# The head of one diffusion layer written out by hand, with tokens 0-767 ahead of the others

## The chip, the cores and the metric

The kernel runs on one core of a Trainium2 chip. A core has five engines with an instruction queue each: TensorE (PE, matmuls and transposes; its weight loads are listed as PEld), VectorE (DVE), ScalarE (ACT), GpSimd (POOL) and SyncE (SP), which here issues most of the DMA transfers. SBUF is the memory on the chip, 128 partitions wide; PSUM holds what TensorE writes. The metric is the device time of one execution in microseconds, lower is better.

## The reference

One inference step of a layer, on 1024 latent tokens and 128 context tokens with 1024 channels, all in fp32:

```python
mod = silu(c) @ w_ada + b_ada          # one row for latent, one for context tokens: sh1, sc1, ga1, sh2, sc2, ga2
h = rmsnorm(x, g1) * (1 + sc1) + sh1
u, q, k, v, g = split(h @ w_in)        # 512, 1024, 256, 256, 2048 columns
m = sigmoid(g_f) * (fourier_mix(u) @ w_fo) + sigmoid(g_a) * (attention(q, k, v, cache, sink) @ w_ao)
x = x + ga1 * (m @ w_out)
h = rmsnorm(x, g2) * (1 + sc2) + sh2
x = x + ga2 * (square(relu(h @ w_ff1)) @ w_ff2)     # 4096 hidden channels
y = rmsnorm(x, final_g)
```

Attention reads a window of 128 tokens to either side and the cached context keys; context tokens read only each other. The outputs are y for both kinds of tokens and the new keys and values.

## The kernel before

The tokens are nine tiles of 128: tiles 0 to 7 are latent, tile 8 is context. The 1024 channels are eight chunks of 128. A product in fp32 is made of three matmuls on operands that are split into a high and a low part (high by high, high by low, low by high); a split is an ACT cast (L147 and others) and a DVE subtraction (L142).

**The head.** The nine x tiles are loaded by SP (L408, 512 KB each), squared and summed on ACT (L410) and normalised in groups of three (the small steps L177 to L183, then the multiplications L417 on DVE and L415 on POOL). TensorE transposes each tile in eight pieces of 128 x 128 (L422), which ACT and DVE copy out of PSUM (L423). Then, chunk by chunk (`make_h`): the chunk's columns of `w_ada` are loaded in two halves (L401), multiplied by silu(c) on TensorE (L436 for chunk 0 in one fp32 piece, L449 for the others, split), the result row is copied (L458), turned into columns by four small matmuls (L462, "fold"), the bias is added on DVE (L464, L467), and the chunk of all 1152 tokens is modulated on ACT (L471), cast (L472) and its low part subtracted (L142). Projection round 1 multiplies tiles 0 to 5 by the first 512 columns of `w_in` chunk by chunk (L233 to L235, 144 matmuls of 512 columns); round 2 does tiles 6 to 8, after the results of round 1 have been copied out (L365). Here a scheduler sets the order of each engine's queue, by data dependences and estimated costs.

**The middle.** Projections, the Fourier mixer and attention follow, in an order written out by hand (`tc.manual_schedule`). Meanwhile the other modulation chunks are made a piece at a time and added up on DVE (L282) into `mods`, which holds them with the channel on the partition.

**The modulation rows.** The gate vectors ga1 and ga2 are wanted as rows along the free axis on all partitions. `ga_rows` (L1238) writes them from `mods` to a DRAM buffer `ga_d`, two channel chunks at a time, eight transfers on POOL's queue for each gate; each transfer writes single fp32 elements. It is called for ga1 ahead of the seam, and for ga2 at unit 12 of the first MLP matmul (FF1); the scheduler lets each transfer go when its part of `mods` is ready. `ga_put` (L1359) loads a row spread over 128 partitions.

**The seam.** Between w_out and the MLP each tile is finished in steps: `fin_a` multiplies the output by ga1, adds it to the residual row in one of three buffers `XS[t % 3]`, stores that row to DRAM and sums its squares (L1427 to L1434); `fin_b1`, `fin_b2` make the reciprocal root; `fin_b3` scales the row on ACT (L1461); `fin_c` transposes it (L1473) and modulates it (L1478 on ACT, L1480 on DVE). Tile 5 is scaled in place in `XS[2]`. Pieces of other work (`part`, `ev_part`, `t_hi`, `t_lo`) are dealt between these steps in a written order.

**FF1.** Units of weights of 2 x 512 KB are loaded through SP (L1379) into two rotating buffers, split on ACT and DVE, and multiplied (L1684 to L1686); the results go to DRAM through SP as well (L1356), so loads and stores stand in one queue.

## Time and profile before

| what | value |
|---|---|
| median of 3 runs (lowest to highest) | 1657.26 us (1656.18 to 1659.58) |
| profiled execution | 1654.63 us, span 1652.9 us |
| mean granted TensorE clock | 0.995 |
| busy PE / DVE / ACT / POOL | 1610.2 / 1127.1 / 884.8 / 273.1 us |
| DMA | 290.19 MB, mean 176 GB/s |
| first transpose of the head | at 11.51 us |
| first matmul of projection round 2 | at 86.86 us |

The profiled execution is one run under the hardware profiler; the span goes from its first to its last instruction. A row of the timeline gives start, duration, engine, line, operation, operands, and in brackets the engine's idle time before it with what released it. A matmul's duration overlaps the next one's, so the distance between starts is its price in a sequence. The granted clock is the share of full speed at which TensorE was allowed to run in a stretch.

### The profile page before, as it was taken

Reading aid. Unit: us, or ns where it says so; the run is one execution under the profiler, and the core shown is the slowest. Engines: PE = TensorE matmul, PEld = TensorE weight load, DVE = VectorE, ACT = ScalarE, POOL = GpSimd, SP = SyncE. Lnnn points to the kernel's source line nnn. Section 1 sums busy time; section 2 is a strip of 40 time slices with the busy share of each in tenths; the row PEclk is TensorE's granted clock in tenths of the full one; section 3 lists DMA queues with packets and bytes.
Section 4 is the critical chain, followed back from the end, with each engine's and each line's share of the span. In section 5 each row is a group of like instructions: output and inputs, shape, how many; then the busy total and the mean of one; then the engine's idle time right before and its main releaser. Section 6 shows DMA issues by size and latency. Waiting matters only on the chain.

```text
span 1652.9 us, 24756 instructions
## 1 busy us (share of the span) xinstructions
PE 1610.2 (97%) x8357; PEld 1412.5 (85%) x8357; DVE 1127.1 (68%) x2215; ACT 884.8 (54%) x1722; POOL 273.1 (17%) x399
## 2 busy tenths in 40 slices
PE   6999999999999999999999999999999999999998
PEld 5789889899889999889988888887888888888887
DVE  7644266867767865678658877766776588785764
ACT  7743455777677665564346564444445354444542
POOL 1020252555445332310000000000000200000000
PEclk9999999999999999999999999999999999999999
DMA  8342578556444333587575335445555995666841
GB/s 322 129 121 87 182 215 216 132 119 162 121 125 114 106 106 112 160 285 237 161 288 178 117 138 183 163 146 143 166 146 180 348 375 176 197 202 188 257 155 64
DMA packets 217351, 290.19 MB, mean 176 GB/s; under 512 B 27540, under 2 KB 142164, under 8 KB 217096
## 3 DMA queue, kind: packets, MB, share of 16 engines
q1 hardware_dynamic: 205768, 269.72, 52.6%
q0 software_dynamic: 11456, 18.90, 4.0%
q8 instruction: 66, 1.08, 0.3%
q14 instruction: 61, 0.50, 0.1%
HBM read 205.10 MB, written 83.44 MB: 175 GB/s over the span
## 4 chain that ended last, share of the span: by engine, by line
PE 74%; DVE 5%; DMA 3%; ACT 2%; issue 1%; SPq 0%; DVEq 0%; ACTq 0%
PE x L2083 6%; PE x L2085 6%; PE x L2084 6%; PE x L1684 5%; PE x L1686 5%; PE x L1685 5%; PE mm L195 4%; PE mm L197 4%; PE mm L196 4%; PE ptp L859 3%; PE x L197 2%; PE x L195 2%; PE x L196 2%; PE s L819 2%; PE s L820 2%; PE o L874 2%
## 5 line engine op out<-in xcount | busy, mean ns | idle before, releaser
L142 DVE TENSOR_TENSOR wlo<-wraw,whi 128x1024 fp32r<-128x1024 f32 x96 | 121.4, 1266 | 97.8 <-ACT whi L147 75.2
L833 ACT ACTIVATE pt<-pt,mx 128x513 f32<-128x513 f32 (+2 forms) x144 | 95.8, 666 | 82.9 <-DVE mx L821 64.5
L196 PE MATMUL mm<-BR,whi 128*128 128x384 f32 x408 | 137.1, 336 | 0.0
L2084 PE MATMUL x<-BR 128*128 128x512 f32 (+1 forms) x348 | 132.9, 382 | 0.0
L2085 PE MATMUL x<-BR 128*128 128x512 f32 (+1 forms) x348 | 132.5, 382 | 0.0
L2083 PE MATMUL x<-BR 128*128 128x512 f32 (+1 forms) x348 | 131.4, 382 | 0.0
L195 PE MATMUL mm<-BR,whi 128*128 128x384 f32 x360 | 128.1, 356 | 2.9 <-ACT z L717 1.6
L821 DVE CUSTOM_DVE_ANT_0 pt<-s,mask,nsink 128x512 f32<-128x512 f32 (+2 forms) x144 | 96.7, 673 | 40.4 <-PE s L820 38.2
L845 POOL TENSOR_SCALAR pt<-pt,mx 128x512 f32<-128x512 f32 (+2 forms) x144 | 94.8, 670 | 177.5 <-DVE mx L843 175.7
L197 PE MATMUL mm<-BR,wlo 128*128 128x384 f32 x360 | 121.6, 338 | 0.0
L147 ACT CAST whi<-wraw 128x1024 fp32r<-128x1024 f32 x62 | 64.9, 1049 | 100.1 <-DMA wraw<-in_w_ff_dram 53.7
L2056 ACT CAST BR<-aa 128x512 fp32r<-128x512 f32 x80 | 49.7, 621 | 105.5 <-PE x L2084 51.4
L142 DVE TENSOR_TENSOR pl<-ptp,ph 128x512 fp32r<-128x512 f32 x124 | 83.8, 687 | 23.1 <-ACT ph L862 21.7
L326 POOL TENSOR_TENSOR macc<-macc,mprod 128x512 f32<-128x512 f32 x70 | 93.7, 1338 | 7.7 <-ACT macc L324 2.5
L196 PEld LDWEIGHTS mm<-BR,whi 128*128 128x128 f32 x408 | 77.1, 189 | 6.0
L859 PE MATMUL ptp<-ident,pt 128*128 128x128 f32 x496 | 74.4, 274 | 4.0 <-DVE pl L142 3.9
L142 DVE TENSOR_TENSOR BR<-aa,BR 128x512 fp32r<-128x512 f32 x80 | 55.2, 690 | 33.2 <-ACT BR L2056 32.7
L862 ACT CAST ph<-ptp 128x512 fp32r<-128x512 f32 x124 | 70.5, 585 | 12.5 <-PE ptp L859 11.2
L195 PE MATMUL mm<-BT,whi 128*128 128x384 f32 x216 | 76.8, 356 | 0.0
L2084 PEld LDWEIGHTS x<-BR 128*128 128x128 f32 x348 | 65.4, 188 | 12.9
L2083 PEld LDWEIGHTS x<-BR 128*128 128x128 f32 x348 | 65.4, 188 | 12.9
L2085 PEld LDWEIGHTS x<-BR 128*128 128x128 f32 x348 | 65.4, 188 | 12.6
(470 smaller groups left out, 4792.8 us busy)
## 6 DMA issues: line engine op xcount, KB each, us to landing
aa<-hr_d SPq DMA_DIRECT2D x108, 256.0 KB
ab<-in_w_ff_dram SPq DMA_DIRECT2D x108, 256.0 KB
hr_d<-ZR SPq DMA_DIRECT2D x104, 256.0 KB
wraw<-in_w_in_dram SPq DMA_DIRECT2D x41, 512.0 KB
wraw<-in_w_ff_dram SPq DMA_DIRECT2D x34, 512.0 KB
mraw<-in_w_ada_dram SPq DMA_DIRECT2D x96, 128.0 KB
z_d<-z SPq DMA_DIRECT2D x48, 192.0 KB
q_d<-qt SPq DMA_DIRECT2D x48, 192.0 KB
```

The costliest lines, as they stand in the source:

```text
L142: return eng.tensor_tensor(dst, raw, hi.bitcast(F32), ALU.subtract)
L195: nc.tensor.matmul(out, ah, bh, start=start, stop=False)
L196: nc.tensor.matmul(out, ah, bl, start=False, stop=False)
L197: return nc.tensor.matmul(out, al, bh, start=False, stop=stop).ins
L326: nc.gpsimd.tensor_tensor(acc, acc, pr_, ALU.add)
L821: nc.vector.tensor_tensor_reduce(out=pt[:, e, :n], in0=sp[:, :n], in1=mask[:, m0 : m0 + n], scale=-0.125, scalar=nsink[:, h0 + e : h0 + e ...
L833: nc.scalar.activation(pt[:, e, : n + 1], pt[:, e, : n + 1], AF.Exp, bias=mx[:, e : e + 1], scale=-1.0, accum_out=mx[:, 2 + e : 3 + e],)
L845: ins = nc.gpsimd.tensor_scalar(pt[:, e, :n], pt[:, e, :n], mx[:, 4 + e : 5 + e], 1.0, ALU.mult, ALU.mult)
L859: nc.tensor.transpose(pst[:, h * P : (h + 1) * P], u["pts"][h // 2][:, h % 2, b * P : (b + 1) * P], ident)
L2083: nc.tensor.matmul(ps, xh, bh, start=start, stop=False, skip_group_check=cont)
L2084: nc.tensor.matmul(ps, xh, bl, start=False, stop=False, skip_group_check=cont)
L2085: nc.tensor.matmul(ps, xl, bh, start=False, stop=stop, skip_group_check=cont)
```

## The change

1. **Head.** The loops are replaced by a list of steps in a written order for PE, ACT, DVE and SP. Tiles 0 to 5 go first: their six x tiles and the weights for chunks 0 to 2 are loaded ahead of tiles 6 to 8, the x buffers go from nine to six, and silu's copies (`put_c`) stand behind the first loads. The modulation of chunk 0 starts ahead of the first transpose. Tokens 0-767 are modulated, split and multiplied chunk by chunk; for chunk 0 in two pieces of 384. Tiles 6 to 8 are transposed within chunks 3 to 5, and tokens 768-1151 are modulated on POOL (`h3`), split and left for round 2 at the end of chunks 5 and 6. Tiles 4 and 5 are normalised on POOL, and so are 6 to 8.
2. **Modulation rows.** `ga_rows` turns eight chunks by two transposes on TensorE, copies the 8 x 256 result on ACT and writes it with one transfer on SP.
3. **Seam.** Tile 5's scaled row goes to `XS[1]` instead of in place; row 8 is loaded before row 7; tile 7's `fin_b3` moves up ahead of `ev_part` and `fin_c(6)`; `fin_c(7, 0)` takes its PSUM bank from another pool; some `part`, `t_hi` and `t_lo` pieces change places.
4. **Context step.** In `step_ctx` the eight matmuls with the low part of the tokens follow the sixteen others instead of standing between them.

The number of projection, modulation and transposing matmuls is the same, but for the four new transposes of part 2. Lines below are those of the kernel before (L3xx to L19xx) or of the changed one, as marked.

TensorE at the start of the head, before (`x` is a PSUM bank, `xt` an x tile, `wada` modulation weights, `mr` the modulation row; x2 or x4 counts equal rows):

```order
L422 MATMUL x_152<-ident,xt_130 128x128 x4
L422 MATMUL x_158<-ident,xt_130 128x128 x4
...
L422 MATMUL x_244<-ident,xt_198 128x128 x4
L436 MATMUL mm_310<-wada_311,siluc 2x256 x4
L436 MATMUL mm_310<-wada_313,siluc 2x256 x4
L422 MATMUL x_272<-ident,xt_250 128x128 x4
...
L422 MATMUL x_304<-ident,xt_258 128x128 x4
L462 MATMUL mm_325<-ident,mr_323 128x2 x2
L449 MATMUL mm_335<-whi_340,crep 128x256
```

The same in the changed kernel:

```order
L478 MATMUL mm_176<-wada_128,siluc 2x256 x4
L427 MATMUL x_182<-ident,xt_122 128x128 x4
...
L427 MATMUL x_200<-ident,xt_124 128x128 x4
L478 MATMUL mm_176<-wada_130,siluc 2x256 x4
L427 MATMUL x_210<-ident,xt_126 128x128 x4
L427 MATMUL x_215<-ident,xt_126 128x128 x4
L496 MATMUL mm_233<-ident,mr_231 128x2 x2
L427 MATMUL x_248<-ident,xt_132 128x128 x4
...
L427 MATMUL x_281<-ident,xt_134 128x128 x4
L525 MATMUL x_288<-whi_265,BR 128x512
```

The modulation of chunk 0 now brackets the first two tiles, its fold stands behind three tiles instead of nine, and the first projection matmul behind five.

DVE in the changed head, from the multiplication of tile 2 to the low part of the first tokens (`rs_` are the small steps of the reciprocal root):

```order
L457 TENSOR_SCALAR xt_126<-xt_126,rs_r_168 128x1024
...
L488 COPY mr_231<-mm_176 2x256
L500 TENSOR_SCALAR mods<-mm_233,cols 128x2 x2
L501 TENSOR_SCALAR s_94<-mods,cols 128x2
L448 RECIPROCAL rs_a_226<-rs_a_226 128x2
...
L457 TENSOR_SCALAR xt_132<-xt_132,rs_r_227 128x1024
L443 TENSOR_SCALAR rs_v_258<-ssq 128x1
L431 COPY xnT<-x_210 128x4x128
L508 TENSOR_SCALAR xnT<-xnT,s_94,mods 128x384
...
L142 TENSOR_TENSOR wlo_266<-wraw_138,whi_265 128x1024
L142 TENSOR_TENSOR BR<-xnT,BR 128x384
```

In this order tile 3's multiplication stands behind the modulation of chunk 0, and the first projection's low parts behind both.

ACT in the seam around tile 7, before (L1461 scales tile 7, L1478 modulates, L1363 casts, L1714 copies a result):

```order
L1446 ACTIVATE rsw_10107<-rsw_10107 128x1
L1714 COPY ZR<-x_10121 128x384
L1478 ACTIVATE ZR<-mm_10140,mods,s_95 128x128 x4
L1363 CAST BR<-ZR 128x512
L1461 ACTIVATE ZR<-ZR,rsw_10107 128x1024
L1363 CAST BR<-ZR 128x512
```

The changed kernel (L1668 scales):

```order
L1653 ACTIVATE rsw_10146<-rsw_10146 128x1
L1668 ACTIVATE ZR<-ZR,rsw_10146 128x1024
L1921 COPY ZR<-x_10160 128x384
L1685 ACTIVATE ZR<-mm_10180,mods,s_95 128x128 x4
L1570 CAST BR<-ZR 128x512 x2
```

The scaling has moved ahead of a copy, four modulations and a cast.

SP in FF1 of the changed kernel, around the second row store (L1563 stores results, L1586 loads weights):

```order
L1586 DMA wraw_12693<-in_w_ff_dram 128x4x256
L1965 DMA hc_d<-ZR 128x512
L1563 DMA hr_d<-ZR 128x512 x2
L1446 DMA ga_d<-ZR 8x2x128
L1586 DMA wraw_12695<-in_w_ff_dram 128x4x256
L1563 DMA hr_d<-ZR 128x512 x7
L1965 DMA hc_d<-ZR 128x512
L1586 DMA wraw_12862<-in_w_ff_dram 128x4x256
L1586 DMA wraw_12864<-in_w_ff_dram 128x4x256
```

The row store, which was on POOL's queue, stands between two stores and a weight load.

The diff, cut to its core:

```diff
@@ -401,79 +399,286 @@
...
+            def h_id(m, r, vec=None):
+                for a, b, tok in ((r.start, min(r.stop, 1024), 0), (max(r.start, 1024), r.stop, 1)):
+                    if a < b:
+                        x, sc, sh = xnT[:, m, a:b], s1[:, m, tok : tok + 1], mod(0, m, tok)
+                        if vec:
+                            vec.tensor_scalar(x, x, sc, sh, ALU.mult, ALU.add)
+                        else:
+                            nc.scalar.activation(x, x, AF.Identity, bias=sh, scale=sc)
+
+            def h_hi_(m, r):
+                nc.scalar.copy(h_hi[m][:, r], xnT[:, m, r])
+
+            def h_lo_(m, r):
+                sub(nc.vector, h_lo[m][:, r], xnT[:, m, r], h_hi[m][:, r])
+
...
+            R0, R1, R6, R3 = slice(0, 384), slice(384, 768), slice(0, 768), slice(768, NT)
+            ET = mybir.EngineType
+            mh = ExitStack()
+            mh.enter_context(tc.manual_schedule(engines={ET.PE, ET.Activation, ET.DVE, ET.SP}))
+            px = {}
+
+            def xTs(t):
+                for hh in range(2):
+                    px[t, hh] = xT(t, hh, bank6)
+
+            def xevs(t, engs):
+                for hh in range(2):
+                    if engs[hh] != "-":
+                        xev(t, hh, px[t, hh], engs[hh])
+
+            for t in range(3):
+                x_load(t)
+            wada_load(0)
+            for t in range(3, 6):
+                x_load(t)
+            win_load(0)
+            wada_load(1)
+            wada_load(2)
+            win_load(2)
+            put_c()
+            for t in range(3):
+                square(t)
+            rs_a(0, 3)
+            rs_b(0, 3)
+            ada_mv(0, (0,))
+            xmul(0)
+            xTs(0)
+            square(3)
+            xmul(1)
+            xTs(1)
+            ada_mv(0, (1,))
+            xmul(2)
+            xTs(2)
+            xevs(0, "va")
+            square(4)
+            xev(1, 0, px[1, 0], "v")
+            rs_a(3, 2)
+            xev(1, 1, px[1, 1], "a")
+            mod_row(0, True)
+            mod_col(0)
+            square(5)
+            rs_b(3, 2)
+            xmul(4, nc.gpsimd)
+            xmul(3)
+            xTs(3)
+            rs_a(5, 1)
+            xevs(2, "va")
+            win_hi(0)
+            h_id(0, R0, nc.vector)
+            h_hi_(0, R0)
+            rs_b(5, 1)
+            xmul(5, nc.gpsimd)
+            xTs(4)
+            win_lo(0)
+            h_lo_(0, R0)
+            u_mm(0, (0,))
+            ada_hi(1, 0)
+            xevs(3, "aa")
+            ada_lo(1, 0)
+            xTs(5)
+            u_mm(0, (1, 2))
+            ada_hi(1, 1)
+            ada_lo(1, 1)
+            xevs(4, "aa")
+            xevs(5, "va")
+            ada_hi(2, 0)
+            h_id(0, R1, nc.vector)
+            h_hi_(0, R1)
+            h_lo_(0, R1)
+            ada_lo(2, 0)
+            ada_mv(1)
+            mod_row(1)
+            ada_hi(2, 1)
+            for t in range(6, NTT):
+                x_load(t)
+            u_mm(0, (3,))
+            mod_col(1)
+            u_mm(0, (4, 5))
+            h_id(1, R6)
+            h_hi_(1, R6)
+            ada_lo(2, 1)
+            h_lo_(1, R6)
+            ada_mv(2)
+            win_hi(2)
+            win_lo(2)
+            wada_load(3)
+            win_load(4)
+
+            def h3(m):
+                h_id(m, R3, nc.gpsimd)
+                h_hi_(m, R3)
+                h_lo_(m, R3)
+
+            for k in range(1, KC):
+                n = k + 1
+                more = n + 1 < KC
+                tl = k + 3 if k in (3, 4, 5) else None
+                if n < KC:
+                    mod_row(n)
+                u_mm(k, (0,))
+                if n < KC:
+                    mod_col(n)
+                if more:
+                    ada_hi(n + 1, 0)
+                    ada_lo(n + 1, 0)
+                u_mm(k, (1, 2))
+                if tl:
+                    ta = xT(tl, 0, mmt)
+                u_mm(k, (3,))
+                if tl:
+                    tb = xT(tl, 1, mmt)
+                u_mm(k, (4, 5))
+                if n < KC:
+                    h_id(n, R6)
+                    h_hi_(n, R6)
+                if tl:
+                    xev(tl, 0, ta, "a")
+                if more:
+                    ada_hi(n + 1, 1)
+                if n < KC:
+                    h_lo_(n, R6)
+                if tl:
+                    xev(tl, 1, tb, "v")
+                if more:
+                    ada_lo(n + 1, 1)
+                    ada_mv(n + 1)
+                if k in (2, 4):
+                    win_hi(k + 2)
+                    win_lo(k + 2)
+                if k == 2:
+                    win_load(6)
+                if k + 3 < KC:
+                    wada_load(k + 3)
+                if k == 1:
+                    square(6)
+                    square(7)
+                if k == 2:
+                    square(8)
+                    rs_a(6, 3)
+                    rs_b(6, 3)
+                    for t in range(6, NTT):
+                        xmul(t, nc.gpsimd)
+                if k == 5:
+                    h3(0)
+                if k == 6:
+                    for m in range(1, KC):
+                        h3(m)
+            mh.close()
@@ -1233,12 +1438,14 @@
     fbank[0] = gt
 
     def ga_rows(k, row):
+        pr = fold_bank[0]()
         for tok in range(2):
-            for m in range(0, 8, 2):
-                nc.gpsimd.dma_start(
-                    ga_d[row + tok, m * P : (m + 2) * P].rearrange("(m p) -> p m", p=P),
-                    mods[:, k * 8 + m : k * 8 + m + 2, tok],
-                )
+            nc.tensor.transpose(pr[:8, tok * P : (tok + 1) * P], mods[:, k * 8 : k * 8 + 8, tok], ident)
+        rows = zh(3)[:8, : 2 * P]
+        nc.scalar.copy(rows, pr[:8, : 2 * P])
+        nc.sync.dma_start(
+            ga_d[row : row + 2].rearrange("t (m p) -> m t p", p=P), rows.rearrange("m (t p) -> m t p", t=2)
+        )
 
     def ga_load(pool, row, tag):
         out = []
@@ -1457,7 +1664,7 @@
     def fin_b3(t, n=1):
         rs = rsd.pop(t)[2]
         for i in range(n):
-            hs = XS[(t + i) % 3] if t + i == 5 else ys[t + i].rearrange("p k c -> p (k c)")
+            hs = XS[1] if t + i == 5 else ys[t + i].rearrange("p k c -> p (k c)")
             nc.scalar.activation(hs, XS[(t + i) % 3], AF.Copy, scale=rs[:, i : i + 1])
 
     def fin_b(t, n=1):
@@ -1465,10 +1672,10 @@
         fin_b2(t)
         fin_b3(t, n)
 
-    def fin_c(t, kh):
+    def fin_c(t, kh, bank=mmt):
         tok = 0 if t < 8 else 1
-        px = mmt()
-        hn, yt = XS[t % 3] if t == 5 else ys[t].rearrange("p k c -> p (k c)"), ys[t]
+        px = bank()
+        hn, yt = XS[1] if t == 5 else ys[t].rearrange("p k c -> p (k c)"), ys[t]
         for q in range(4):
             nc.tensor.transpose(px[:, q * P : (q + 1) * P], hn[:, (kh * 4 + q) * P : (kh * 4 + q + 1) * P], ident)
         for q in range(4):
@@ -1634,7 +1841,7 @@
     fin_b2(5)
     fin_b3(5)
     fin_c(4, 1)
-    row(7)
+    row(8)
     t_rest_m(1)
     r0, r1 = raws.pop(0)
     u1 = tuple(pz.tile([P, 4, 256], F32R, tag=tag, name=nm(tag), bufs=1) for tag in ("whi", "wlo"))
@@ -1643,7 +1850,7 @@
     t_first(2)
     fin_c(5, 0)
     fin_c(5, 1)
-    row(8)
+    row(7)
     major(2, 3)
     load_wout(2, 5)
     t_rest_m(2)
@@ -1739,6 +1946,8 @@
             wh, wl = wh[:, k % 4], wl[:, k % 4]
             nc.tensor.matmul(ps[:, :256], cth[:, k], wh, start=(k == 0), stop=False)
             nc.tensor.matmul(ps[:, :256], cth[:, k], wl, start=False, stop=False)
+        for k in range(KC):
+            wh = (h0 if k < 4 else h1)[:, k % 4]
             nc.tensor.matmul(ps[:, :256], ctl[:, k], wh, start=False, stop=(k == KC - 1))
         v = zh(4)[:, :256]
         nc.scalar.activation(v, ps[:, :256], AF.Relu)
@@ -1838,35 +2047,35 @@
     ga_put(1)
     part("a", 1, RA, True)
     fin_b2(7)
+    fin_b3(7)
     ev_part(RA)
     fin_c(6, 0)
     fin_c(6, 1)
     part("e", 4, RA, True)
     t_hi(1, 3, y11)
-    fin_b3(7)
     t_lo(1, 3, y11)
     t_hi(2, 3, y21)
     t_lo(2, 3, y21)
-    fin_c(7, 0)
+    fin_c(7, 0, gt)
     fin_c(7, 1)
     nc.vector.tensor_tensor(y11, y12, y11, ALU.subtract)
     t6 = tmpt().rearrange("p (k c) -> p k c", k=4)
     nc.vector.tensor_tensor(t6, y22, y11, ALU.subtract)
+    part("a", 2, RA)
     part("a", 1, RB)
+    nc.vector.tensor_tensor(y12, y22, y12, ALU.subtract)
     ev_part(RB)
-    part("a", 2, RA)
+    t_hi(6, 3, t6)
+    t_lo(6, 3, t6)
+    t_hi(7, 3, y12)
+    t_lo(7, 3, y12)
     nc.scalar.copy(w4v[0], sb)
     sub(nc.vector, w4v[1], sb, w4v[0])
     wu[0]["u4"] = w4v
     ff1_load(1)
+    part("b", 6, RA, True)
     part("a", 2, RB)
-    t_hi(6, 3, t6)
-    t_lo(6, 3, t6)
-    part("b", 6, RA, True)
     part("b", 6, RB)
-    nc.vector.tensor_tensor(y12, y22, y12, ALU.subtract)
-    t_hi(7, 3, y12)
-    t_lo(7, 3, y12)
     t_hi(5, 3, y11)
     step_p7(0)
     uh(1, 1)
```

More of the change, by code (lines that the diff above doesn't have):

```diff
@@ new lines, in win_hi, with win_lo, put_c @@
+            def win_hi(k):
+                hi, lo = (wp.tile([P, 2, 512], F32R, tag=t, name=nm(t), bufs=3) for t in ("whi", "wlo"))
+                win[k] = win[k], hi, lo
+                nc.scalar.copy(hi, win[k][0])
+            def win_lo(k):
+                sub(nc.vector, win[k][2], win[k][0], win[k][1])
+            def put_c():
+                nc.vector.tensor_copy(c4[:, :, :, 0], sil_kt)
+                sub(nc.vector, c4[:, :, :, 1], sil_kt, c4[:, :, :, 0])
+                for k in range(KC):
+                    nc.vector.tensor_copy(
+                        crep[:, k],
+                        c4.bitcast(F32)[:, k].rearrange("p a b -> p (a b)").unsqueeze(1).to_broadcast([P, 32, 4]),
+                    )
@@ new lines, in xT, with xev @@
+            def xT(t, hh, bank):
+                ps = bank()
+                for m in range(4):
+                    mm = hh * 4 + m
+                    nc.tensor.transpose(ps[:, m * P : (m + 1) * P], xts[t][:, mm * P : (mm + 1) * P], ident)
+                return ps
+            def xev(t, hh, ps, eng):
+                (nc.scalar.copy if eng == "a" else nc.vector.tensor_copy)(
+                    xnT[:, hh * 4 : hh * 4 + 4, t * P : (t + 1) * P], ps.rearrange("p (m t) -> p m t", m=4)
+                )
@@ L456, in make_h, with mod_row @@
-                mr = p0.tile([4, 256], F32, tag="mr", name=nm("mr"), bufs=2)
-                nr = 2 if plain else 4
-                nc.scalar.copy(mr[:nr], ps[:nr, 0:256])
-                fold = ident[0:2, 0:2] if plain else pairsum
+                        for i, x in enumerate(wspl[m, hf]):
+                            w = x[:, kk].rearrange("p a n -> p (a n)")
+                            nc.tensor.matmul(ps[:, 0:256], st, w, start=(k == 0 and i == 0), stop=(k == 7 and i == 1))
+            def mod_row(m, vec=False):
+                nr = 2 if m == 0 else 4
+                mr = p0.tile([4, 256], F32, tag="mr", name=nm("mr"), bufs=1)
+                (nc.vector.tensor_copy if vec else nc.scalar.copy)(mr[:nr], mrs[m][:nr, 0:256])
+                mrs[m] = mr
@@ L460, in make_h, with mod_col @@
+            def mod_col(m):
+                nr = 2 if m == 0 else 4
+                fold = ident[0:2, 0:2] if m == 0 else pairsum
                 pt = mmt()
                 for e in range(2):
-                    nc.tensor.matmul(pt[:, 2 * e : 2 * e + 2], mr[:nr, e * P : (e + 1) * P], fold, start=True, stop=True)
+                    nc.tensor.matmul(
+                        pt[:, 2 * e : 2 * e + 2], mrs[m][:nr, e * P : (e + 1) * P], fold, start=True, stop=True
+                    )
                 for e in range(2):
-                    nc.vector.tensor_scalar(
-                        mods[:, e * 8 + m, :], pt[:, 2 * e : 2 * e + 2], cols[:, 16 + e * 8 + m : 17 + e * 8 + m], None, ALU.add
-                    )
```

123 lines of the change are left out of this document (59 added, 64 removed).

## The prediction

> **What bounds the kernel now.** I read the page's busy shares and its chain of waits first.
>
> ```profile
> span 1652.9 us, 24756 instructions
> PE 1610.2 (97%) x8357; PEld 1412.5 (85%) x8357; DVE 1127.1 (68%) x2215; ACT 884.8 (54%) x1722; POOL 273.1 (17%) x399
> PE 74%; DVE 5%; DMA 3%; ACT 2%; issue 1%; SPq 0%; DVEq 0%; ACTq 0%
> ```
>
> TensorE (PE) is busy 97% of the span and carries most of the chain, so a change that leaves its matmuls alone can only win PE's idle time (1652.9 − 1610.2 = 42.7 us) and the time that PE ran at a lowered clock. The table of windows says where both lie in the three stretches that the change touches: head up to the first matmul of round 2, seam, FF1 with everything behind it.
>
> ```profile
> 11.50:86.86 75.36, 68.70 (x377) 56.27 (x377) 50.50 (x80) 54.89 (x77) 4.12 (x4) 0.98 0.57 201
> 815.00:970.00 155.00, 152.41 (x762) 129.62 (x761) 112.59 (x235) 83.79 (x159) 3.19 (x6) 1.00 0.51 176
> 970.00:1645.00 675.00, 672.33 (x3186) 564.47 (x3185) 474.53 (x788) 304.85 (x520) 15.74 (x24) 1.00 0.61 192
> ```
>
> The columns are length, busy time of PE, its weight loads, DVE, ACT, POOL, then granted clock. Idle PE is 6.7 us of the head, 2.6 of the seam, 2.7 of the rest; another 11.5 pass before the first transpose. These are the ceilings of the parts.
>
> **Head.** PE's waits up to 160 us (total, times, longest) and its timeline:
>
> ```profile
> PE x L422 <- DVE xt L417: 9.0, 2, 8.0
> PE mm L462 <- ACT mr L458: 1.8, 2, 1.0
> PE x L233 <- ACT BT L472: 1.5, 1, 1.5
> 11.51 5.14 PE L422 MATMUL x<-ident,xt 128*128 128x128 f32 x24 [7.96 <-DVE xt L417]
> 20.43 3.62 PE L436 MATMUL mm<-wada,siluc 128*2 128x256 f32 x16
> 23.98 2.84 PE L422 MATMUL x<-ident,xt 128*128 128x128 f32 x24
> 26.75 0.60 PE L462 MATMUL mm<-ident,mr 2*128 2x2 f32 x4
> 27.28 0.39 PE L449 MATMUL mm<-whi,crep 128*128 128x256 f32 x1
> 29.15 0.28 PE L449 MATMUL mm<-wlo,crep 128*128 128x256 f32 x1
> 78.50 0.39 PE L234 MATMUL x<-wlo,BT 128*128 128x512 f32 x1
> 78.72 1.52 PE L235 MATMUL x<-whi,BT 128*128 128x512 f32 x6
> 86.86 0.50 PE L233 MATMUL x<-whi,BR 128*128 128x512 f32 x1 [0.79 <-ACT u L365]
> ```
>
> A step costs what lies between starts. Transposes: (26.75 − 23.98)/24 = 0.115 us. The plain modulation matmuls of chunk 0: (23.98 − 20.43)/16 = 0.222, 3.6 in all. A fold: 27.28 − 26.75 = 0.53. A later chunk's sixteen modulation matmuls: (29.15 − 27.28) + 0.12 = 2.0. A projection matmul: (1.52 − 0.39)/5 = 0.226. The work up to round 2 is therefore 72 × 0.115 + 3.6 + 7 × 2.0 + 8 × 0.53 + 144 × 0.226 = 62.7 us, the same after the change except that 24 transposes move into it elsewhere. It took 75.4 from the first transpose, so 12.7 were lost: 6.7 idle, the rest to a clock that was still low (24 transposes in 5.14 us where 2.8 would do) or fell again.
>
> The new order lets PE start before the normalisation. What it waits for at each point:
>
> ```profile
> 6.79 1.06 ACT L410 ACTIVATE sq<-xt 128x1024 bf16<-128x1024 f32 x1 [0.16 <-DMA xt<-in_x_lat_dram]
> 8.07 1.06 ACT L410 ACTIVATE sq<-xt 128x1024 bf16<-128x1024 f32 x1
> L417 DVE TENSOR_SCALAR xt<-xt,rstd x6: 735/807/1616, 10.7 to 22.0; 128x1024 f32<-128x1024 f32 x6
> 10.85 1.58 POOL L415 TENSOR_SCALAR xt<-xt,rstd 128x1024 f32<-128x1024 f32 x1 [6.92 <-ACT sq L410]
> L464 DVE TENSOR_SCALAR mods<-mm,cols 128x2 f32<-128x2 f32 x16 | 2.7, 212 | 6.0 <-PE mm L462 6.0
> L142 DVE TENSOR_TENSOR wlo<-wraw,whi 128x1024 fp32r<-128x1024 f32 x9 | 10.9, 1222 | 12.7 <-ACT whi L147 12.7
> 29.90:33.30 3.40, 1.95 (x13) 1.67 (x13) 2.53 (x5) 3.40 (x5) 0.00 (x0) 1.00 0.52 195
> 33.30:36.75 3.45, 3.05 (x9) 2.21 (x8) 2.93 (x4) 3.45 (x5) 0.00 (x0) 0.51 0.67 213
> ```
>
> Loads of 512 KB land 1.28 apart (6.79 to 8.07, the second and third x tile). The first half of the modulation weights is now the fourth load: 8.07 + 1.25 = 9.3, and PE begins there, 2.2 earlier. Eight plain matmuls at half pace end at 12.8; DVE's three multiplications from 10.7 are ready by then; 16 transposes at 0.213 (5.14/24) end at 16.2, the second half of chunk 0's modulation at 18.0, tile 2 at 18.9. Then PE is short of work: copy of the row 0.3, fold 0.53, three small DVE steps 0.65, five rsqrt steps of 0.2 and the multiplication of tile 3 (0.75) bring the next transposes to 21.8, a hole of about 2.5. Behind the multiplication DVE has an evacuation 0.6, the modulated tokens 0-383 0.5, rsqrt 0.9, the weights' low part 1.2 and the tokens' low part 0.5: the first complete projection group can run at 25.6. POOL multiplies tiles 4 and 5 beside that: the slowest L417 took 1.616 against 0.735 next to POOL's 1.58, so I add one such delay, 0.9. Left for PE at 26.5 are 32 transposes, seven modulation chunks and folds, and 143 matmuls: 3.7 + 14.0 + 3.7 + 32.3 = 53.7. With 1.3 for small waits and part of a lowered clock, round 2 starts at 81.5 instead of 86.86: **−5.4**. Bounds: no delay by POOL and no waits, 25.6 + 53.7 = 79.3, with some of the early DVE work cheaper 78.5 (−8.4); all 5.6 us of the later waits of before (6.7 without the 1.04 at the transposes) plus 1.7 of half clock, 26.5 + 53.7 + 7.3 = 87.5 (+0.6). I take a value nearer the low end because the splits of the next chunk's weights are now spread between PE's groups. Evacuations, casts and splits are the same work; what hides them is these 53.7 us of PE, with DVE 50.5 of 75.4 busy before. If that cover fails, they return as waits of about 1 us each. Tokens 768-1151 are modulated on POOL during the last chunk, 0.6 us each against 9 × 0.226 = 2.0 of PE per chunk in round 2.
>
> [...]
>
> **Modulation rows.** The sixteen element stores of L1238 go, eight in the attention stage, eight in FF1.
>
> ```profile
> L1238 POOL DMA_DIRECT2D ga_d<-mods x16: 706/723/784, 317.6 to 1232.4; - x16
> DMA to landing us min/median/max: 9.0/9.7/10.2
> 1135.80 1.42 POOL L1238 DMA_DIRECT2D ga_d<-mods  x2 [61.56 <-DVE mods L282]
> 1140.00:1146.00 6.00, 6.00 (x32) 5.10 (x31) 1.61 (x4) 2.07 (x4) 0.00 (x0) 1.00 1.03 99
> 1140.65 0.38 SPq L1379 DMA_DIRECT2D wraw<-in_w_ff_dram  x1
> 1149.86 1.04 ACT L147 CAST whi<-wraw 128x1024 fp32r<-128x1024 f32 x1 [6.63 <-DMA wraw<-in_w_ff_dram]
> 1152.43 0.51 PE L1684 MATMUL x<-ER,BT 128*128 128x512 f32 x1 [2.67 <-ACT BT L1402]
> 1152.90:1156.33 3.43, 3.43 (x10) 2.68 (x9) 3.04 (x5) 1.36 (x3) 0.00 (x0) 0.50 0.36 82
> ```
>
> The two stores of 1135.8 are still out until about 1146; in that time the DMA engines are occupied throughout (share 1.03) and move 99 GB/s. The weight load issued at 1140.65 lands only at 1149.8, the casts follow, PE stands 2.7 us and runs 3.43 us at half clock: 2.7 + 1.7 = **−4.4**. In their place come four transposes (4 × 0.115 = **+0.5**), two ACT copies and two stores in SP's order. Stores of 16 rows of 512 bytes are not in the trace of before; the nearest, SP's ordinary stores, show no such freeze. PE's transposes wait for the modulation's last step, each pair at most as long as the longest wait of a transposing step in the seam (1.0, quoted below): +2 at worst. If the load was late for another reason, the 4.4 stays: bounds −4.4 and +2.5, and I take the low end because of the 99 GB/s. The attention-stage stores cost PE nothing that I can see, so nothing is counted there.
>
> **Seam.** Two transposing steps wait for the ACT scaling of tiles 5 and 7.
>
> ```profile
> PE mm L1473 <- ACT ZR L1461: 1.8, 2, 1.0
> 900.51 1.15 ACT L1461 ACTIVATE ZR<-ZR,rsw 128x1024 f32<-128x1024 f32 x1 [2.69 <-DMA x_d<-ZR]
> 931.76 0.62 ACT L1363 CAST BR<-ZR 128x512 fp32r<-128x512 f32 x1
> 932.29 1.14 ACT L1461 ACTIVATE ZR<-ZR,rsw 128x1024 f32<-128x1024 f32 x1
> ```
>
> Tile 5 is scaled in place, so it waits for the store of its residual; written to another buffer it starts up to 2.69 us earlier, and the 0.96 wait goes. Tile 7's scaling moves ahead of a copy, four modulations and a cast (order, part on the change), and the 0.83 goes. **−1.8**, at best −2.6 (all idle time of the seam), at worst +1 where tile 7's row, now loaded second, or the copy ACT does later is missed. The eight matmuls of the context step only change places: nothing.
>
> **Sum.** −5.4 − 4.4 + 0.5 − 1.8 = −11.1 on the span of 1652.9; the profiled execution took 1654.63, the median is 1657.26, so I forecast 1646.2, say **1646 us**.
>
> **Rivals.** (A, 0.60) As summed; its own range, from the bounds that go together, is 1641 to 1650. (B, 0.15) The head wins nothing: the later waits return while the hole at 19 to 22 takes the clock. For it: DVE stands between all its steps; against: 2.2 us of earlier start and 6.7 of idle time to win. −5.7: 1651.5. (C, 0.07) The late load at 1140 isn't due to the element stores; for it, ACT waited for weight loads elsewhere too; against, the 99 GB/s. −6.7: 1650.5. (D, 0.08) Both: −1.3, 1656. (E, 0.10) Slower by FF1's weight loads.
>
> ```profile
> 1142.55 9.23 SPq L1356 DMA_DIRECT2D hr_d<-ZR  x2
>   ACT whi L147: 53.7, 19
> ```
>
> SP issues in order; two stores kept it 9.23 us, and ACT stood 53.7 us before 19 of the 32 loads of L1379. FF1's order is dealt anew by the scheduler, the new row store stands in SP's order ahead of a weight load, and in one place seven stores now stand ahead of two loads in a row. Each load that comes late enough costs the 4.4 of the one seen. Two such loads undo 8.8 of 11.1; from three on the kernel is slower, 1657.26 − 11.1 + 4 × 4.4 = 1664 for four. Against it: in the trace one of 32 loads went that far.
>
> **How the numbers follow.** Medians of this kernel differ by about 0.2% (3.3 us) without a change, so faster means below 1654: A, B and C make 0.82, and a little of D 0.02; the same 0.06; slower 0.10. The range runs from 1639.5 (head −8.4, rows −3.9, seam −2.6 is −14.9, 1642.4, with 2.9 for what a freer DMA may give elsewhere) to 1653, leaving D and E out.
>
> **What would show it.** First matmul of PE near 9.3 and round 2 near 81.5; no PE wait over 1 us around 1150 and no half clock there; no wait of L1473's successor for the scaling. Wrong if PE idles more than 6 us between 20 and 80, if a weight load of FF1 ends a PE wait of 2 us again, or if the time goes where no part touched.

## The result and the profile after

The changed kernel took 1646.09 us (median of 4 runs, 1643.85 to 1648.28), the kernel before 1656.93 (4 runs): ratio 0.9936, 95% interval 0.9918 to 0.9953. The forecast was 1646. In two later measurements, on two chips where the kernel before took 1661 to 1662, the same changed kernel stood at 0.9908 (0.9892 to 0.9924) and 0.9911 (0.9896 to 0.9927), so the gain was 10.8 us in the first measurement and about 15 in the later ones. The chip of the first is not known. That the forecast met the first of these is not yet a proof of its terms: the rest of this document shows that two of the three had another size, and that the third is not resolved.

The changed kernel's profiled execution took 1648.12 us. Its page, span, busy time and chain:

```profile
span 1646.3 us, 24742 instructions
PE 1611.3 (98%) x8361; PEld 1411.8 (86%) x8361; DVE 1129.8 (69%) x2228; ACT 883.1 (54%) x1726; POOL 283.4 (17%) x401
PE 81%; DVE 3%; DMA 1%; ACT 1%; issue 1%; SPq 0%; DVEq 0%; ACTq 0%
```

PE's idle time has fallen from 42.7 to 35.0 us. The span is only 6.6 shorter, less than the times say. PE's waits in the changed kernel, behind its first modulation matmul and up to 160 us:

```profile
PE x L427 <- DVE rs_v L443: 2.4, 1, 2.4
PE mm L483 <- DVE alo L142: 0.8, 1, 0.8
```

Some rows of its timeline, from the first modulation matmul to the first matmul of round 2:

```profile
9.99 3.57 PE L478 MATMUL mm<-wada,siluc 128*2 128x256 f32 x8 [6.57 <-DVE rs_r L449]
21.29 3.65 PE L427 MATMUL x<-ident,xt 128*128 128x128 f32 x16 [2.44 <-DVE rs_v L443]
24.58 0.78 PE L525 MATMUL x<-whi,BR 128*128 128x512 f32 x1
27.37 0.47 PE L525 MATMUL x<-whi,BR 128*128 128x512 f32 x1
83.91 0.50 PE L233 MATMUL x<-whi,BR 128*128 128x512 f32 x1
```

And three windows (length; busy PE, weight loads, DVE, ACT, POOL; clock, DMA share, GB/s):

```profile
20.30:27.20 6.90, 5.92 (x25) 5.51 (x26) 6.69 (x14) 5.88 (x10) 3.95 (x2) 0.51 0.88 330
27.37:83.91 56.54, 55.16 (x308) 45.21 (x307) 40.58 (x66) 41.52 (x60) 20.40 (x19) 1.00 0.47 150
970.00:1285.00 315.00, 315.00 (x1562) 266.19 (x1561) 222.07 (x356) 147.29 (x230) 5.68 (x9) 1.00 0.50 165
```

The hole of the forecast is there (2.44 us ahead of tile 3's transposes), the clock falls to 0.51 in it (from 20.30) and stays there for 6.9 us, and round 2 begins at 83.91: 2.95 earlier than before, not 5.4. Over the profiles of the next section round 2 begins at 83.6 to 84.1 with this head (six profiles) and at 86.9 to 88.3 with the old one (five), 3.6 earlier on average. FF1 has no idle time up to 1285. In the seam a wait appeared that the kernel before did not have (timeline of SP and PE; L1766 loads the rows, L1724 the w_out weights):

```profile
898.03 0.33 SPq L1766 DMA_DIRECT2D ZR<-in_x_lat_dram  x1
906.35 0.42 SPq L1724 DMA_DIRECT2D whi<-wo_d  x1
913.23 0.50 PE L1622 MATMUL x<-whi,BT 128*128 128x512 f32 x1 [2.30 <-DMA whi<-wo_d]
```

The window behind it:

```profile
914.00:918.00 4.00, 4.00 (x12) 3.09 (x11) 2.52 (x3) 0.73 (x2) 0.00 (x0) 0.58 0.18 68
```

The two waits for the scaling, 1.8 in all, are gone, but a pair of w_out loads, issued at 906 behind tile 7's row, landed after PE wanted it: 2.3 us, and 1.7 of half clock.

### The profile page after: what moved, and what is told of

Same layout as the page of the kernel before. It is cut to its first block, busy times and chain, and to the rows that moved or that the text cites. A ratio compares the mean times of both kernels' runs of the same rounds, so it can differ in the third digit from the quotient of the medians.

```text
span 1646.3 us, 24742 instructions
## 1 busy us (share of the span) xinstructions
PE 1611.3 (98%) x8361; PEld 1411.8 (86%) x8361; DVE 1129.8 (69%) x2228; ACT 883.1 (54%) x1726; POOL 283.4 (17%) x401
## 4 chain that ended last, share of the span: by engine, by line
PE 81%; DVE 3%; DMA 1%; ACT 1%; issue 1%; SPq 0%; DVEq 0%; ACTq 0%
PE x L1891 6%; PE x L1892 6%; PE x L1893 6%; PE x L2292 6%; PE x L2293 6%; PE x L2294 6%; PE mm L195 4%; PE mm L197 4%; PE mm L196 4%; PE ptp L1064 3%; PE x L197 2%; PE x L195 2%; PE x L196 2%; PE x L1622 2%; PE x L1624 2%; PE x L1623 2%
## 5 line engine op out<-in xcount | busy, mean ns | idle before, releaser
L147 ACT CAST whi<-wraw 128x1024 fp32r<-128x1024 f32 x58 | 60.9, 1050 | 84.1 <-DMA wraw<-in_w_ff_dram 39.7
L1067 ACT CAST ph<-ptp 128x512 fp32r<-128x512 f32 x124 | 70.7, 586 | 12.2 <-PE ptp L1064 10.8
L2292 PEld LDWEIGHTS x<-BR 128*128 128x128 f32 x348 | 65.4, 188 | 13.0
L2293 PEld LDWEIGHTS x<-BR 128*128 128x128 f32 x348 | 65.4, 188 | 12.8
```

Source lines behind the costliest of these rows:

```text
L2292: nc.tensor.matmul(ps, xh, bh, start=start, stop=False, skip_group_check=cont)
L2293: nc.tensor.matmul(ps, xh, bl, start=False, stop=False, skip_group_check=cont)
```

## The experiments

Each row of the table is one profile and 4 to 11 executions; the changed kernel has three rows. To read the profiles against each other, the table gives the length of three stretches, each from the first start of a kind of matmul to that of the next: from the start to the first score matmul of the attention (head and what follows it), from the first w_out matmul to the first of FF1 (seam), from there to the first of FF2, the second MLP matmul (FF1).

| kernel | median us | ratio to before (95%) | to scores | seam | FF1 |
|---|---|---|---|---|---|
| before (profile shown first) | 1656.93 | 1 | 274.7 | 105.1 | 366.2 |
| changed (first measurement) | 1646.09 | 0.9936 (0.9918 to 0.9953) | 272.4 | 107.7 | 360.6 |
| head alone | 1654.73 | 0.9967 (0.9956 to 0.9979) | 271.6 | 106.0 | 370.1 |
| rows alone | 1651.03 | 0.9942 (0.9929 to 0.9956) | 274.9 | 106.5 | 361.7 |
| seam and context step alone | 1662.47 | 1.0011 (1.0002 to 1.0020) | 277.5 | 103.8 | 373.1 |
| rows of ga2 alone | 1652.64 | 0.9950 (0.9933 to 0.9967) | 275.5 | 107.4 | 361.8 |
| changed, again | 1645.81 | 0.9908 (0.9892 to 0.9924) | 272.5 | 103.8 | 360.6 |
| changed, third time | 1647.06 | 0.9911 (0.9896 to 0.9927) | 270.8 | 105.2 | 360.6 |
| changed without seam | 1646.31 | 0.9911 (0.9896 to 0.9926) | 272.5 | 105.1 | 361.8 |
| changed without head | 1649.96 | 0.9936 (0.9919 to 0.9953) | 275.6 | 105.5 | 360.6 |
| changed, tile 7's row held back | 1643.82 | 0.9897 (0.9882 to 0.9913) | 272.3 | 106.7 | 360.6 |
| changed, tile 3 first | 1646.01 | 0.9913 (0.9899 to 0.9928) | 272.9 | 105.0 | 360.6 |
| both of these | 1645.51 | 0.9906 (0.9892 to 0.9921) | 272.3 | 106.6 | 360.6 |
| start dealt anew, row held back | 1645.01 | 0.9897 (0.9882 to 0.9913) | 273.2 | 103.8 | 360.6 |

The kernels from "head alone" to "seam alone" and the one with the row held back share one chip's runs of before (1660.42, 20 runs). The second row of the changed kernel, the rows of ga2 alone, tile 3 first and the one with both edits share another chip (1662.25, 11 runs); the third row of the changed kernel, those without seam and without head and the one with the start dealt anew a third (1660.92, 11 runs).

**The head alone.** The kernel before with the first two hunks of the diff.

```diff
-            ps_u = tok_proj_round(ROUNDS[0], 0, bank6, None, before=make_h)
+            mh.enter_context(tc.manual_schedule(engines={ET.PE, ET.Activation, ET.DVE, ET.SP}))
...
```

> The kernel before with the new head alone. Theory (the parts add up, and the head's gain is what the trace of the changed kernel shows at the first matmul of round 2, 2.95 us earlier, and 2.2 us earlier at 270 us): 2 to 4 us less than before; hole of about 2.4 us in PE near 19, half clock from 20 to 27, round 2 near 83.9. Rival (the head was worth the 5.4 forecast and something else ate it): 5 to 6 us less, round 2 near 81.5. Rival (nothing is carried past the attention stage): no change to the end.

Measured: 0.9967, 5.5 us less (3.5 to 7.3). The trace has the hole and round 2 at 84.0. The time alone would have fitted the forecast, the trace does not: the gain at round 2 is 3 to 4. In the nine profiles with the new head or a variant of it the scores begin at 272.3 on average, in the five with the old one at 275.6, a difference of 3.3 (2.9 without the latest of the five, 277.5). With the stores gone as well (changed with and without the head, ratios 0.9911 and 0.9936) the head is worth 4.1 by the ratios and 2.9 by the medians. So the head gives 3 to 5 us.

This kernel keeps the element stores, and FF1 took 8.4 us more than with rows alone. PE's waits there, and the window in which the stores of 1131 are under way:

```profile
PE x L1889 <- ACT BT L1607: 4.0, 1, 4.0
```

```profile
1130.00:1140.00 10.00, 10.00 (x54) 8.59 (x54) 6.55 (x15) 4.31 (x8) 1.41 (x2) 1.00 0.63 74
```

Its weight load behind the stores of 1131 came later than in the kernel before: PE waited 4.0 instead of 2.7.

**The rows alone.**

```diff
-                nc.gpsimd.dma_start(
-                    ga_d[row + tok, m * P : (m + 2) * P].rearrange("(m p) -> p m", p=P),
...
+            nc.tensor.transpose(pr[:8, tok * P : (tok + 1) * P], mods[:, k * 8 : k * 8 + 8, tok], ident)
...
+        nc.scalar.copy(rows, pr[:8, : 2 * P])
+        nc.sync.dma_start(
...
```

> The kernel before with the modulation rows turned by TensorE alone. Theory (the element stores froze the DMA engines at 1140, and the late weight load cost 2.7 of wait and 1.7 of half clock): 4 us less, no PE wait over 1 us in FF1, no half clock near 1153. Rival (the late load has another cause): the wait of 2.7 stays or moves by some us, and the time is within 1 us of before.

Measured: 0.9942, 9.6 us less (7.3 to 11.8): twice the forecast's 3.9. The rival falls, since FF1 shows no idle time up to 1285 (window of the kernel with the rows alone):

```profile
970.00:1285.00 315.00, 315.00 (x1576) 267.07 (x1575) 223.15 (x358) 149.40 (x235) 5.64 (x9) 1.00 0.49 165
```

**The seam and the context step alone.** The hunks for `XS[1]`, the row order, `fin_c`, the `part` order and `step_ctx`:

```diff
-            hs = XS[(t + i) % 3] if t + i == 5 else ys[t + i].rearrange("p k c -> p (k c)")
+            hs = XS[1] if t + i == 5 else ys[t + i].rearrange("p k c -> p (k c)")
...
-    row(7)
+    row(8)
...
```

> The kernel before with the seam's changes and the context step's order alone. Theory (the two waits for the scaling go, but the third pair of w_out loads now shares the DMA engines with tile 7's row and lands late in some executions): single executions of two kinds, some 2 us under before without the wait for those loads, some 2 us above with it (2.5 of wait, 1.7 of half clock). Rival (the wait at 910 us in the changed kernel comes from the earlier arrival of everything else): no wait there, 1.8 us less than before in all.

Measured: 1.0011, 1.8 us more (0.3 to 3.3). Both expectations missed: the seam itself took 103.8, 1.3 less than before, with no wait for w_out loads. Against the profile of before, 6.9 us were lost in FF1, where the element stores still are, and 2.8 ahead of the scores, where this edit changes nothing. Its timeline on POOL, SP and ACT around the last pair of stores:

```profile
1229.54 1.41 POOL L1238 DMA_DIRECT2D ga_d<-mods  x2 [41.66 <-DVE mods L282]
...
1230.03 0.38 SPq L1379 DMA_DIRECT2D wraw<-in_w_ff_dram  x1
...
1246.12 1.04 ACT L147 CAST whi<-wraw 128x1024 fp32r<-128x1024 f32 x1 [8.16 <-DMA wraw<-in_w_ff_dram]
```

PE's waits in its FF1:

```profile
PE x L1686 <- DVE wlo L142: 6.0, 1, 6.0
PE mm L1754 <- ACT ZR L1747: 2.4, 1, 2.4
```

And two windows:

```profile
1235.00:1240.00 5.00, 5.00 (x33) 4.55 (x32) 1.88 (x2) 2.96 (x5) 0.00 (x0) 1.00 0.64 38
1250.00:1255.00 5.00, 0.16 (x1) 0.16 (x1) 3.43 (x5) 1.05 (x1) 0.00 (x0) 0.54 0.66 240
```

The last pair of stores goes out at 1229.5, a weight load 0.5 later, and that load is there only at 1246, 16 us on. The DMA engines move 38 GB/s meanwhile, from 1235 to 1240. PE waits 8.4 us and works on at half clock (0.54 from 1250 to 1255, 0.50 from 1255 to 1260). Against 361.7 (old seam) or 360.6 (new seam) without the stores, FF1 took 4.4 more in the profile of before, 8.4 with the head alone and 12.5 here. These are three profiles of three kernels, the first from the first measurement. The times give a similar order: turning the rows saves 9.6 on the kernel before, 9.3 with the new head (0.9967 and 0.9911) and 12.5 with the new seam (1.0011 and 0.9936), the last two across chips and each within some 3 us. If the price were drawn anew between 4.4 and 12.5 in each execution, single executions would scatter with a standard deviation of about 4 us, an estimate from the three figures; on this chip it is 1.9 (before), 1.6 (head alone) and 1.5 (seam alone), no more than with the rows alone (1.9). So the price seems to differ by kernel, or by chip, rather than by execution; one profile of each doesn't settle it.

**The rows of ga2 alone**, to see whether the eight stores of the attention stage have a price too. The kernel before, with the new function, here under another name, for the second call only:

```diff
-            ga_rows(5, 2)
+            ga_rows_t(5, 2)
```

> The kernel before with the new way for the rows of ga2 alone (the eight element stores of FF1 gone, the eight of the attention stage kept). Theory (all the price of the element stores lies in FF1, where a weight load is late by a different amount in each execution): the same gain as with both rows turned, 8 to 10 us, and no PE wait over 1 us in FF1. Rival (the stores in the attention stage cost as much): 4 to 5 us, half of it.

Measured: 0.9950, 8.3 us less (5.5 to 11.1), beside 9.6 for both. By the times the theory holds within the intervals: FF1 carries most of it. But the stores of the attention stage are not free, as this kernel's own profile shows. The first row is of PE, then follow two windows of this kernel:

```profile
397.48 0.47 PE L819 MATMUL s<-kth,qT 128*128 128x512 f32 x1 [1.93 <-DVE mods L282]
372.00:376.00 4.00, 4.00 (x29) 3.84 (x28) 1.53 (x5) 2.84 (x8) 3.92 (x6) 1.00 0.58 14
396.80:403.60 6.80, 6.12 (x24) 5.64 (x25) 4.70 (x15) 2.46 (x8) 1.75 (x3) 0.75 0.43 116
```

The same windows with both rows turned (rows alone):

```profile
372.00:376.00 4.00, 4.00 (x28) 3.74 (x28) 2.14 (x7) 3.52 (x9) 3.92 (x5) 1.00 0.74 177
396.80:403.60 6.80, 6.80 (x43) 6.44 (x42) 4.64 (x13) 4.83 (x12) 4.10 (x6) 1.00 0.47 120
```

Behind the last pair of stores (369.4 and 370.2) the DMA engines move 14 GB/s instead of 177, the next loads of modulation weights are issued at 383.3 instead of 377.8, and PE waits 1.93 us for the modulation sums and runs on at a lowered clock: 3.6 us from the scores to w_out, 450.2 against 446.6. The seam alone has the same wait (1.57 at 399); before and the head alone have the stores and no such wait, and none of the ten profiles without these stores has it. Two of this kernel's six executions, the profiled one among them, took 1656 to 1658 and the other four 1650 to 1653, which would fit a price that comes in some executions only; the other executions have no trace.

**The changed kernel twice more, then without the seam's hunks and without the head's.** For the last two the diff is the whole change without the part named.

> The changed kernel unaltered, beside the others on one chip. Theory (parts add up, as measured apart on the chip of the earlier runs: head -5.5, rows -9.6, seam +1.8): 11 to 14 us less than before, single executions in two groups some 4 us apart, as the w_out loads near 910 are late or not. Rival (the late w_out loads of the one profile were an accident): one group, within 1 us of the kernel with tile 7's row held back.

> The changed kernel unaltered once more, as the measure for the three beside it: 11 to 15 us less than before.

> The changed kernel with the seam and the context step as before (head and rows alone). Theory (the seam's edits win the two scaling waits, 1.8, and in half the executions lose 2 to 4 to late w_out loads, so they come out near nothing; the 1.8 that they cost alone on the kernel before came from the element stores): within 1.5 us of the changed kernel, waits of about 1 us for the scaling of tiles 5 and 7 in the profile. Rival (the seam's edits cost 1.8 anywhere): about 2 us less than the changed kernel. Rival (they win as forecast): about 2 us more.

> The changed kernel with the head as before (rows, seam and context step alone). Theory (the head is worth 3 to 5.5): 3 to 5.5 us more than the changed kernel. Rival (the head's gain belongs to executions with element stores in the attention stage only): within 1.5 us of it.

Measured: the changed kernel 0.9908 and 0.9911; its executions spread from 1642.1 to 1649.4 without two clear groups, so the theory of two kinds of execution is not borne out, though the late loads come and go (below). Without the seam's edits 0.9911, with them 0.9911 on the same chip. The waits that they remove are there again in the seam of the kernel without them (PE's waits):

```profile
PE mm L1680 <- ACT ZR L1668: 1.7, 3, 0.8
```

What replaces them differs by execution. In profiles with the new seam PE waited for the w_out loads 2.3, 0, 1.0 (the changed kernel three times), 0 (seam alone), 1.5 (without head) and 1.0 us (tile 3 first, below). Tile 7's part of the gain is steady: FF1, which begins ahead of that wait, is 1.1 us shorter (360.6 against 361.7 or 361.8) in every pair of profiles without element stores. Timing does not resolve it: within about 3 us the edits are worth nothing in sum. The head, as said, is worth 2.9 to 4.1 here.

**Tile 7's row held back.** One column of the row's buffer is set on DVE behind the third pair; the row then overwrites it, so its load has to wait (it was issued at 910.98, behind the third pair at 907.24 and 907.61, where the changed kernel issued it at 898.03).

```diff
     fin_c(5, 0)
     fin_c(5, 1)
-    row(7)
     major(2, 3)
...
     load_wout(2, 6)
+    nc.vector.memset(XS[1][:, 0:1], 0.0)
+    row(7)
```

> The changed kernel with tile 7's row loaded behind the third pair of w_out loads instead of ahead of the second (a one-column store to its buffer holds it back). Theory (the row's 512 KB make the pair late): no PE wait for the w_out loads near 910, no half clock there, all executions near 1644, none near 1648. Rival (the pair is late by itself, one DMA engine lagging): the wait stays in the profile or in half of the executions, median still 1646.

Measured: 0.9897, and no wait for the w_out loads near 910 in this profile nor in the two others that hold the row back; the four executions lie between 1642.2 and 1645.3. That agrees with the theory for the wait, but does not prove it: of the six profiles that don't hold the row back two have no such wait either. And the seam was not shorter (106.7, 106.6 and 103.8 in the three profiles against 103.8 to 107.7): waits of about 1 us for earlier w_out loads, near 840, came in two of them, and the kernel with both edits, on another chip, is at 0.9906. Its gain over the changed kernel is not established. It was tried again only together with other edits.

**Tile 3 first at the start of the head.**

```diff
-            mod_row(0, True)
-            mod_col(0)
             square(5)
             rs_b(3, 2)
-            xmul(4, nc.gpsimd)
             xmul(3)
+            xmul(4, nc.gpsimd)
+            mod_row(0, True)
             xTs(3)
+            mod_col(0)
```

> The changed kernel with tile 3's rsqrt steps and multiplication ahead of chunk 0's row copy on DVE, and tile 3's transposes ahead of the fold on PE; nothing else moves. Theory (the hole near 19 us comes from this DVE order, and the half clock from 20 to 27 from the hole): no PE wait over 1 us between 17 and 25, first complete projection group 1 to 2 us earlier, no half clock or one window less, round 2 3 to 4 us earlier than in the changed kernel, and as much off the time. Rival (later waits for the weights' low parts take it back): round 2 less than 1.5 us earlier. Rival (the clock falls anyway, since PE does little before 17): one half-clock window stays and the gain is 2.

> Both edits: tile 3 first in the head, tile 7's row held back in the seam. Theory (independent places): the sum of both, 15 to 20 us less than before and the fastest of all. Rival (the head's gain is absorbed by waits in the attention stage): as the kernel with tile 7's row held back alone.

Measured: 0.9913 alone, 0.9906 with the row held back, both like the changed kernel. Round 2 began at 85.3 and 84.2, where 3 to 4 us earlier than the changed kernel's 83.6 to 83.9 was expected. PE's timeline with tile 3 first:

```profile
18.76 1.07 PE L427 MATMUL x<-ident,xt 128*128 128x128 f32 x8 [0.32 <-DVE xt L457]
...
23.18 0.50 PE L525 MATMUL x<-whi,BR 128*128 128x512 f32 x1 [1.80 <-ACT BR L513]
24.21 0.80 PE L526 MATMUL x<-wlo,BR 128*128 128x512 f32 x1 [0.54 <-DVE wlo L142]
```

The hole of 2.4 was filled, and one of 1.8 + 0.5 opened three steps later, ahead of the first projection matmul, because DVE does the same steps in another order and the modulation of chunk 0 is now the later one. The clock fell behind that hole too (0.50 from 24 to 30). So the order of these two steps alone does not make the hole. What is left is the whole chain of steps on DVE, which is busy 2.19 of the 2.44 us of the changed kernel's hole; no run takes work off it, so this is argued and not shown.

**The start dealt anew.** Tile 3's rsqrt ahead of the row copy, the first weights' low part ahead of tile 5's rsqrt, tile 5's transposes behind the first three projection groups; tile 7's row held back as above.

```diff
+            rs_b(3, 2)
             mod_row(0, True)
+            xmul(3)
+            xmul(4, nc.gpsimd)
+            win_hi(0)
             mod_col(0)
...
+            win_lo(0)
+            h_lo_(0, R0)
+            u_mm(0, (0,))
+            ada_hi(1, 0)
+            rs_b(5, 1)
+            xmul(5, nc.gpsimd)
...
             u_mm(0, (1, 2))
+            xTs(5)
```

> The changed kernel with tile 7's row held back and the start of the head dealt anew: tile 3's rsqrt ahead of the row copy, the first weights' low part ahead of tile 5's rsqrt, tile 5's transposes behind the first three projection groups. Theory (DVE's chain to the first complete projection group bounds the start; three small steps of it now run while DVE was idle): first complete group near 23 instead of 25.6, round 2 1.5 to 2 us earlier than in the changed kernel, the time 1 to 2 us under it. Rival (moved waits come back, as with tile 3 ahead alone): round 2 not earlier, the same time.

Measured: 0.9897, the same as with the row held back alone. Timeline of PE:

```profile
22.42 0.50 PE L525 MATMUL x<-whi,BR 128*128 128x512 f32 x1 [0.58 <-ACT BR L513]
25.02 0.40 PE L527 MATMUL x<-whi,BR 128*128 128x512 f32 x1
27.57 1.13 PE L427 MATMUL x<-ident,xt 128*128 128x128 f32 x8 [2.15 <-POOL xt L459]
```

The first three groups are done at 25.4 instead of 29.0, as the theory wanted, and then PE waits 2.15 us for tile 5, whose multiplication now stands behind them on POOL. Round 2 began at 85.1. So the rival was right: three orders of the same DVE and POOL work each leave a hole of 2 to 2.5 us between 18 and 28, each with a half clock in or behind it (0.51 from 20.3 to 27.2 in the changed kernel, 0.50 from 24 to 30 and from 29 to 31 in the two others). In the last of them the wait ends on POOL. None of the versions beats the changed kernel beyond doubt.

## Why the prediction was right, step by step

The time was right, and so were its sign and the mechanisms of the head and the stores, but the terms had other sizes. That their sum met the time of the first measurement is in part luck: measured apart later the terms make −12.9, and the whole came to about −15 in the later measurements.

| term | forecast | measured |
|---|---|---|
| head | −5.4 | −3.6 at round 2 and −3.3 at the scores by the profiles; −5.5, −4.1 and −2.9 by the times |
| element stores out, transposes in | −3.9 | −9.6 (7.3 to 11.8) |
| seam | −1.8 | 0 (±3) on the changed kernel, +1.8 (0.3 to 3.3) alone |
| sum | −11.1 | −10.8 in the first measurement, about −15 in two later ones |

In the first measurement the parts were not run apart. Its two profiles differ by −2.2 up to the scores, −1.2 from there to w_out, +2.6 in the seam, −5.6 in FF1 and −0.2 behind it. Whether the stores cost 9.6 there as well, or nearer the 4.4 of its profile, stays open.

**Element stores: right mechanism, mis-sized term.** "2.7 + 1.7 = −4.4" was taken from one profiled execution, in which one load was caught for 2.7 us. Of the three kernels with a profile and these stores it was the cheapest (4.4, 8.4, 12.5). The rival that the late load has another cause fell: in the eleven profiles with the new way for ga2, no wait between 970 and 1285 is longer than 0.42 us. "The attention-stage stores cost PE nothing" held in the profile of before and in that of the head alone, but not in two others (waits of 1.93 and 1.57). The added transposes and the store on SP's queue cost nothing that could be seen; rival E, late weight loads from the new order, did not occur in any profile.

**Head: nearly right up to 27 us, then too hopeful.** PE began at 9.99, not near 9.3. The first complete group was forecast for 26.5; with the other two matmuls of that step and tile 5's transposes behind it, the next would start at about 27.9. The trace has 27.37 for it, by two errors against each other: DVE had the tokens' low part at 24.8, 1.7 us earlier, and the half clock lasted 6.9 us where I had counted on a part of the 3.45 seen in the kernel before. The delay by POOL that I put at 0.9 came only behind the first group. It shows in these two rows of the timeline, one of POOL and one of DVE:

```profile
23.33 2.36 POOL L459 TENSOR_SCALAR xt<-xt,rs_r 128x1024 f32<-128x1024 f32 x1 [1.21 <-ACT BR L513]
24.71 3.20 DVE L142 TENSOR_TENSOR alo<-wada,ahi 128x1024 fp32r<-128x1024 f32 x2
```

Two subtractions took 3.20 where one takes 1.22 elsewhere, 0.8 more. (The forecast added "one such delay, 0.9" from the slowest L417 of the kernel before; that trace has two, 1.616 and 1.615 against 0.735.) What failed is the price of the projection matmuls. Behind 27.37 there are 52.4 us of work by the paces of the forecast (24 transposes 2.8, seven chunks 14.0 and folds 3.7, 141 matmuls 31.9), and it took 56.5. The window row above shows 1.4 of the 4.1 us as idle, so "1.3 for small waits" was about right. From start to start the folds took 3.7 as forecast, the chunks 15.5 with 1.1 of the idle time in them, the transposes 2.2, but the 141 matmuls 35.2 with 0.3 of idle time in them: 0.25 each, where 0.226 is the pace within a row of six. In the kernel before they take 0.24 from 36.75 to round 2, without the idle time. A matmul next to one of another kind takes 0.31 to 0.40 in the changed kernel, whose order alternates the kinds.

**Seam: the waits went as forecast, their time did not stay won.** The waits for both scalings are gone from the profile, and tile 7's 1.1 us are seen in FF1. The bound "at worst +1 where tile 7's row, now loaded second, is missed" looked at the wrong victim: the row was in time, and w_out loads issued behind its 512 KB were not, in four of the six profiles that load it there (waits of 2.3, 1.0, 1.5 and 1.0 us).

**Clock.** In the hole of 2.44 us (18.85 to 21.29) the clock fell to 0.51 and stayed there to 27.20, as the window rows of the kernel before had suggested (PE busy 1.95 of 3.40 us, then 0.51 from 33.30 to 36.75). The 1.7 of half clock in the forecast's upper bound is 3.45 × 0.49 of that row; the same estimate for this fall is 6.9 × 0.49 = 3.4. Near 427 us the changed kernel waits 2.0 to 2.3 us in each of its three profiles, and behind it the clock falls in some executions and not in others. In all fourteen profiles this wait is 2.0 to 2.4 us, and in nine of them the clock falls; here the first and the second profile of the same kernel, window 429 to 434:

```profile
429.00:434.00 5.00, 4.63 (x19) 4.26 (x20) 4.25 (x9) 2.68 (x6) 0.38 (x2) 0.66 0.62 179
```

```profile
429.00:434.00 5.00, 4.57 (x27) 4.26 (x28) 4.75 (x10) 3.13 (x8) 0.38 (x2) 1.00 0.60 177
```

That is 1.7 us in one execution and nothing in the other. No run here shows what decides between the two. With the w_out loads (0 to 2.3, and 1.7 more where the clock falls, 0.58 from 914 to 918) it accounts for most of the 6.1 us by which the two profiles' spans differ (1646.3 and 1640.2), and the first profile, which fell on the bad side of both, helped to make the gain look like 6.6.

What stays open: why the seam's edits alone made the kernel 1.8 us slower (12.5 us for the stores beside the new seam, by the profile and by the times, against 9.6 on the kernel before would explain it, but the intervals overlap), and why the kernel before is 4 to 5 us slower in the later measurements than in the first, where the changed kernel is not. A price of the element stores that varies from chip to chip would explain the second; it was not measured apart.

## What to carry to other kernels

Price a stall that comes from a collision (a transfer caught behind another) from several profiles, not from one: here three kernels gave 4.4, 8.4 and 12.5 us for the same stores. Beside stores of single fp32 elements a weight load was there only 9.2 us after its issue in the kernel before (1140.65 to 1149.86) and 16.1 with the seam alone (1230.03 to 1246.12); turning such a column into a row on TensorE first was the largest single gain here (9.6 us). Price a matmul in the order in which it will run, since 0.226 us became 0.25 where the kinds alternate. And when a hole moves instead of closing as steps are reordered, suspect the engine that does those steps; taking work off it is the next thing to try, and was not tried here.

## What was not expected of the hardware

A weight load of 512 KB was there only after 16 us beside two stores of 256 elements each (1230.0 to 1246.1), with the DMA engines at 38 GB/s in a window between. And behind a TensorE wait of 2.0 to 2.4 us at one and the same place the clock falls in nine profiles (0.66 from 429 to 434 in the changed kernel's first) and stays at full speed in five (1.00 from 429 to 434 in its second).
